# A segment mean on four engines: the instruction order comes from a list scheduler run at build time instead of from slots written by hand

## The chip, the cores and the metric

The kernel runs on one core of a Trainium2 chip. The metric is the device time of one execution in microseconds (us); smaller is better. Engines are named as in the profile: DVE is the VectorE, ACT the ScalarE, POOL the GpSimd, SP the engine whose queue starts the loads, PE the TensorE (hardly used here). "Busy" does not count instructions that only wait, branch or start a transfer. Every engine has its own list of instructions, written when the program is built. In the three traces that were set beside it (the changed kernel, `lat_p35`, `l6p35`) POOL's 90 gathers and ACT's 180 sums come in the order of that list, as far as the trace tells them apart, and an engine whose next instruction is not ready stands idle.

## The reference

```python
def setup_inputs():
    n = 10_000_000
    num_segments = 10000
    return {"data": np.random.randn(n).astype(np.float32),
            "segment_ids": np.sort(np.random.randint(0, num_segments, n))}     # int64

def reference(data, segment_ids):
    num_segments = int(segment_ids.max()) + 1
    sums = np.zeros(num_segments, dtype=np.float32)
    counts = np.zeros(num_segments, dtype=np.float32)
    np.add.at(sums, segment_ids, data)
    np.add.at(counts, segment_ids, 1)
    return sums / np.maximum(counts, 1)
```

The ids are sorted, so a segment is a contiguous stretch of about 1,000 values. The kernel does not have to read the 80 MB of ids, only to find where they change.

## The kernel before

The values lie as 128 partitions of 78,125. A partition is worked off in 90 "rows" of 875 columns (the last is shorter). A row of a partition normally holds one place where the id changes, its *cut*. Two instructions do the work on each row:

```python
def total(r):                                  # ACT: the sum of the row
    ...
    nc.scalar.activation(out=junk_a[:, 0:n], in_=d, func=ACT.Copy, accum_out=t)

def split(r):                                  # DVE: the sum of what lies before the cut
    ...
    nc.vector.scalar_tensor_tensor(
        out=junk_v[:, 0:n], in0=iota[:, 0:n], scalar=KK[:, r : r + 1], in1=d,
        op0=ALU.is_lt, op1=ALU.mult, accum_out=A[:, r : r + 1])
```

The data come in 45 tiles of two rows (875 KB each), through 18 buffers; a buffer is free when both `total` and `split` of its two rows have run. `split(r)` needs the cut `KK[:, r]`, and finding the cuts is a chain through three engines and the transfers:

1. A small load (a "probe") brings every 175th id of an even row, and DVE computes from it which stretch of 175 ids holds the change (`probes_of`, which writes the address `IDX`).
2. POOL gathers those 175 ids of each partition (`gather`, an indirect DMA into one of 18 ring slots).
3. ACT sums them (`add_ids`).
4. DVE turns the sum into the cuts of the even rows (`even_cut`).
5. The cut of an odd row is sought halfway between the cuts of its even neighbours: DVE computes that address (`between`, which writes `IDXO`),
6. POOL gathers 208 ids there, ACT sums them, and DVE writes the odd cuts (`odd_cut`).

```python
def even_cut(a, b):
    def s1():
        add_ids(asked[False, b - 1] + 1)       # ACT sums all gathers up to this one
        nc.vector.scalar_tensor_tensor(out=rows_of(a, b), in0=YY[:, a:b], scalar=float(S // K),
                                       in1=GS[:, a:b], op0=ALU.mult, op1=ALU.subtract)
    ...
def between(c, d):
    def s1(): nc.vector.tensor_add(out=SM[:, c:d], in0=rows_of(c, d), in1=rows_of(c + 1, d + 1))
    def s2(): nc.vector.scalar_tensor_tensor(out=IDXO[:, c:d], in0=SM[:, c:d], scalar=0.5,
                                             in1=FB[:, c:d], op0=ALU.mult, op1=ALU.add)
    ...
def odd_cut(c, d):
    def s1():
        add_ids(asked[True, d - 1] + 1)
        nc.vector.tensor_sub(out=KK[:, 2 * c + 1 : 2 * d : 2], in0=YO[:, c:d], in1=GSO[:, c:d])
```

The even rows are handled in nine groups, `EVEN = [3, 3, 3, 3, 6, 6, 6, 6, 6]`, with the odd rows between them; seven late rows are done by step 1 to 4 alone. In the kernel before, all of these steps are put into slots behind given rows, by hand:

```python
def chain(k):
    c, d = odds(k)
    e, b = even_cut(bounds[k], bounds[k + 1]), between(c, d)
    return e + b[:2] + [lambda: gather(True, c, d)] + b[2:]
...
put(11, chain(3), 4)                           # from row 11, four steps a row
put(13, ask(4, 3, 6))                          # gathers of even rows, in blocks of three
...
for k in range(4, NG):
    b = 2 * bounds[k]
    ...
        put(b - 24, ask(k, 0, 3))
        put(b - 19, ask(k, 3, 6))
    if k >= 5:
        put(b - 9, chain(k), 3)
    put(b - 2, odd_cut(c, c + 3))
    put(b + (1 if k == NG - 1 else 3), odd_cut(c + 3, d))
...
for r in range(-3 - X_DATA, NR):               # the loop that writes the program
    while moves and moves[0][0] <= r + X_DATA: ...      # loads, 26 rows ahead
    if r >= 0:
        add_ids(due(r))                        # sums that a rough rule takes to be there
    while nt < NR and nt <= r + ahead(r):
        total(nt); nt += 1
    if r >= 0:
        split(r)
    for f in after[r]:
        f()
```

## Time and profile before

| | before |
|---|---|
| time, median of three runs (range) | 200.46 us (199.81 to 201.47) |
| span of the profiled execution | 199.7 us |
| busy DVE / ACT / POOL | 143.1 / 138.2 / 99.7 us |
| transfers | full until about 160 us |
| DVE work still to do at 160 us | 31.7 us |

From the page of the kernel before, the busy totals and the rows that show the span in 40 slices of 5 us (a digit is the busy share of a slice in tenths):

```profile
PE 1.6 (1%) x6; PEld 1.4 (1%) x6; DVE 143.1 (72%) x501; ACT 138.2 (69%) x362; POOL 99.7 (50%) x121
...
DVE  6415387931865832979396999994689999949991
...
DMA  5999999999999999999999999999999954000000
```

No engine is full. The transfers are, until slice 32 (about 160 us), and DVE is full only after that: it fell behind while the data came in. The windows view of the same kernel gives this in numbers. Its columns are: window, length, busy us (and instructions) of PE, PEld, DVE, ACT and POOL, granted clock, mean share of the DMA engines, GB/s read.

```profile
0.00:27.00 27.00, 0.00 (x0) 0.00 (x0) 12.47 (x66) 16.79 (x35) 17.53 (x36) 1.00 0.98 237
...
60.00:100.00 40.00, 0.99 (x4) 0.93 (x4) 25.31 (x90) 27.96 (x80) 23.49 (x25) 1.00 1.06 368
100.00:130.00 30.00, 0.00 (x0) 0.00 (x0) 27.77 (x96) 24.44 (x69) 15.94 (x16) 1.00 1.05 372
130.00:160.00 30.00, 0.00 (x0) 0.00 (x0) 24.46 (x77) 20.33 (x55) 14.57 (x15) 1.00 1.01 401
160.00:215.00 55.00, 0.59 (x2) 0.50 (x2) 31.70 (x100) 28.12 (x70) 12.34 (x16) 1.00 0.10 26
```

The DMA share is at about 1 in every window to 160 us, and DVE is busy 77.5 of the 100 us between 60 and 160 (25.31 + 27.77 + 24.46). The waits view says what the engines were waiting for (engine, tile and line, the releaser, then us in total, times, longest):

```profile
POOL GT L342 <- ACT junk_a L445: 40.4, 9, 10.5
ACT junk_a L356 <- DMA GT<-in_segment_ids_dram,IDXO: 28.2, 16, 5.9
...
DVE q L437 <- ACT junk_a L356: 13.0, 4, 4.7
DVE q L437 <- issue: 10.6, 3, 7.0
DVE q L368 <- ACT junk_a L356: 9.5, 6, 4.9
...
DVE q L437 <- ACT junk_a L445: 4.0, 1, 4.0
```

L342 is the gather, L356 the id sum, L445 `total`, L368 and L437 the even and the odd cut. POOL stood 40 us before gathers, ACT stood 28 us before gathered ids that had not landed, and DVE stood 37.7 us in some 15 waits before cuts (the four lines shown, and 0.6 more).

Where ACT really waited for a gather (20 of the 90), the time from the start of POOL's gather to the start of the sum was 6.64 us in the median, by the timelines of POOL and ACT. POOL itself is busy only 1.0 us with a gather and starts the next 1.30 us after it. The Trainium skill ("Perfetto Trace Analysis", DMA Instruction — SWDGE (GPSIMD)) explains why these two differ: the profiler ends such an instruction when its descriptors are written, not when the data have moved. This trace agrees: 1.0 us against 6.64.

### The profile page before, as it was taken

To read this page: it belongs to the slowest core of one execution; us is meant where nothing else is said; L and a number is where in the kernel's file an instruction comes from. 1 tells how busy PE (TensorE), PEld (TensorE's weight loads), DVE (VectorE), ACT (ScalarE), POOL (GpSimd) and SP (SyncE) were. 2 spreads that over 40 slices of the span, in tenths; PEclk is the share of its full clock that TensorE was granted. 3 is DMA by queue.
4 is the path that set the end of the run, shared out by engine and by line. 5 is a ranking of instruction groups with operands and counts; after the bars stand their busy time and mean duration, and the time that the engine had idled before them with its cause. 6 is when DMAs were issued, how large, how long until landed. Compare 5 with 4: busy or idle time off the path is not lost.

```text
span 199.7 us, 1544 instructions
## 1 busy us (share of the span) xinstructions
PE 1.6 (1%) x6; PEld 1.4 (1%) x6; DVE 143.1 (72%) x501; ACT 138.2 (69%) x362; POOL 99.7 (50%) x121
## 2 busy tenths in 40 slices
PE   0000000000000010000000000000000000010000
PEld 0000000000000010000000000000000000010000
DVE  6415387931865832979396999994689999949991
ACT  8556387444946935988499949694996199899900
POOL 5675745750376277617770776367403778602000
DMA  5999999999999999999999999999999954000000
GB/s 67 301 270 289 273 291 195 300 259 333 349 345 350 363 345 360 354 348 412 401 405 399 332 335 358 405 412 406 402 411 423 358 151 124 11 0 2 0 0 11
DMA packets 49781, 55.67 MB, mean 279 GB/s; under 512 B 39632, under 2 KB 40200, under 8 KB 49767
## 3 DMA queue, kind: packets, MB, share of 16 engines
q1 hardware_dynamic: 43835, 40.33, 62.2%
q0 software_dynamic: 5760, 15.22, 23.4%
q14 instruction: 14, 0.11, 0.2%
q10 hardware_dynamic: 172, 0.00, 0.0%
HBM read 57.81 MB, written 0.04 MB: 290 GB/s over the span
## 4 chain that ended last, share of the span: by engine, by line
issue 28%; DMA 24%; SPq 19%; DVE 15%; ACT 9%; POOL 3%; POOLq 0%; ACTq 0%; DVEq 0%
SPq L163 14%; DMA GT<-in_segment_ids_dram,IDXO 10%; DMA data_t<-in_data_dram 10%; DVE junk_v L450 8%; SPq L178 6%; ACT junk_a L356 4%; ACT junk_a L445 4%; DMA GT<-in_segment_ids_dram,IDX 4%; POOL GT L342 3%; DVE sel L781 0%; DVE sel L772 0%; DVE most L869 0%; DVE PS L686 0%; DVE FFP L714 0%; DVE add L861 0%
## 5 line engine op out<-in xcount | busy, mean ns | idle before, releaser
L450 DVE SCALAR_TENSOR_TENSOR junk_v<-iota,q,data_t 128x875 bf16<-128x875 f32 x90 | 100.3, 1115 | 0.3
L445 ACT ACTIVATE junk_a<-data_t 128x875 bf16<-128x875 f32 x90 | 83.6, 929 | 17.7 <-DMA data_t<-in_data_dram 14.3
L342 POOL DMA_INDIRECT GT<-in_segment_ids_dram,IDXO x41 | 41.3, 1007 | 54.5 <-ACT junk_a L445 39.1
L342 POOL DMA_INDIRECT GT<-in_segment_ids_dram,IDX x49 | 49.3, 1005 | 17.8 <-issue 12.4
L356 ACT ACTIVATE junk_a<-GT 128x175 bf16<-128x175 int32 (+1 forms) x90 | 33.5, 372 | 33.2 <-DMA GT<-in_segment_ids_dram,IDXO 28.2
L437 DVE TENSOR_TENSOR q<-YO,GSO 128x3 f32<-128x3 f32 (+1 forms) x14 | 2.3, 162 | 27.6 <-ACT junk_a L356 13.0
L356 ACT ACTIVATION_READ_ACCUMULATOR junk_a<-GT 128x1 f32 x90 | 16.8, 187 | 0.0
L445 ACT ACTIVATION_READ_ACCUMULATOR junk_a<-data_t 128x1 f32 x90 | 16.8, 186 | 0.0
L368 DVE SCALAR_TENSOR_TENSOR q<-YY,GS 128x6 f32<-128x6 f32 (+1 forms) x9 | 1.5, 164 | 10.2 <-ACT junk_a L356 9.5
L450 DVE DVE_READ_ACCUMULATOR junk_v<-iota,q,data_t 128x1 f32 x90 | 7.4, 83 | 0.0
L295 DVE CAST VV<-pr 128x12 f32<-128x12 int32 (+1 forms) x9 | 1.7, 185 | 6.1 <-DMA pr<-in_segment_ids_dram 6.1
L861 POOL TENSOR_TENSOR xa<-pa,RG 128x528 f32<-128x528 f32 x1 | 1.3, 1251 | 8.3 <-DVE RG L858 8.3
L194 ACT ACTIVATE GT<-q 128x3744 int32<-128x3744 f32 x1 | 3.5, 3527 | 0.0
L708 DVE TENSOR_TENSOR q<-T,q 128x44 f32<-128x44 f32 (+3 forms) x4 | 0.7, 181 | 3.4 <-ACT junk_a L445 3.3
L311 DVE TENSOR_SCALAR FE<-ST 128x6 f32<-128x6 f32 (+2 forms) x10 | 1.9, 191 | 0.2
L320 DVE SCALAR_TENSOR_TENSOR IDX<-ST,wb 128x6 int32<-128x6 f32 (+2 forms) x11 | 1.7, 161 | 0.2
L194 ACT ACT_TABLE_LOAD x1 | 1.3, 1283 | 0.7 <-PEq L1070 0.7
L374 DVE TENSOR_SCALAR q<-q 128x6 f32<-128x6 f32 (+1 forms) x9 | 1.5, 171 | 0.3
L416 DVE TENSOR_TENSOR SM<-q 128x6 f32<-128x6 f32 (+2 forms) x9 | 1.5, 165 | 0.3
L325 DVE SCALAR_TENSOR_TENSOR YY<-ST,SG 128x6 f32<-128x6 f32 (+2 forms) x10 | 1.7, 170 | 0.0
L316 DVE TENSOR_TENSOR ST<-ST,FE 128x6 f32<-128x6 f32 (+2 forms) x10 | 1.6, 160 | 0.1
L427 DVE SCALAR_TENSOR_TENSOR YO<-VV,SR 128x6 f32<-128x6 f32 (+2 forms) x9 | 1.5, 171 | 0.2
(151 smaller groups left out, 62.2 us busy)
## 6 DMA issues: line engine op xcount, KB each, us to landing
data_t<-in_data_dram SPq DMA_DIRECT2D x44, 875.0 KB
GT<-in_segment_ids_dram,IDX POOLq DMA_INDIRECT x49
pr<-in_segment_ids_dram SPq DMA_DIRECT2D x42, 6.0 KB
GT<-in_segment_ids_dram,IDXO POOLq DMA_INDIRECT x41
data_t<-in_data_dram SPq DMA_DIRECT2D x1, 437.5 KB
data_t<-in_data_dram SPq DMA_DIRECT2D x1, 125.0 KB
out_dram<-OUT SPq DMA_DIRECT2D x1, 36.6 KB
pt<-in_segment_ids_dram SPq DMA_DIRECT2D x2, 11.0 KB
```

What stands on the lines that cost most here:

```text
L163: nc.sync.dma_start(out=pr[:, a:b, :], in_=bass.AP(ids_p.tensor, ids_p.offset + 2 * L * a, [list(ids_p.ap[0]), [2 * L, b - a], [S, K + 1]]),)
L178: nc.sync.dma_start(out=d[:, 0 : c - a], in_=data_p[:, a:c])
L194: nc.scalar.activation(out=gt32[:, :, 0 : 2 * WO : 2], in_=view(q5[:, 0, 0:1], [[0, RING], [0, WO]]), func=ACT.Copy)
L295: v.tensor_copy(out=VV[:, 2 * a : 2 * b].rearrange("p (a b) -> p a b", b=2), in_=pr32[:, a:b, 0 : 2 * K + 1 : 2 * K],)
L311: v.tensor_scalar(out=FE[:, a:b], in0=ST[:, a:b], scalar1=0.0, scalar2=FAR, op0=ALU.is_equal, op1=ALU.mult)
L320: v.scalar_tensor_tensor(out=IDX[:, c:d], in0=ST[:, c:d], scalar=float(w), in1=wb[:, c:d], op0=ALU.mult, op1=ALU.add)
L325: v.scalar_tensor_tensor(out=YY[:, a:b], in0=ST[:, a:b], scalar=float(K + 1), in1=SG[:, a:b], op0=ALU.mult, op1=ALU.add)
L342: nc.gpsimd.indirect_dma_start(out=GT[:, len(asked) % RING, 0:n], out_offset=None, in_=ids2d[:], in_offset=bass.IndirectOffsetOnAxis(ap=id ...
L356: nc.scalar.activation(out=junk_a[:, 0:n], in_=gt32[:, i % RING, 0 : 2 * n : 2], func=ACT.Copy, accum_out=to[:, r : r + 1],)
L437: nc.vector.tensor_sub(out=KK[:, 2 * c + 1 : 2 * d : 2], in0=YO[:, c:d], in1=GSO[:, c:d])
L445: nc.scalar.activation(out=junk_a[:, 0:n], in_=d, func=ACT.Copy, accum_out=t)
L450: nc.vector.scalar_tensor_tensor(out=junk_v[:, 0:n], in0=iota[:, 0:n], scalar=KK[:, r : r + 1], in1=d, op0=ALU.is_lt, op1=ALU.mult, accum_ ...
```

## The change

The slots go. The program is now described as tasks (engine, busy time, dependences, a rank that says how urgent it is, and for transfers the time of moving the bytes), and a class `Plan` steps a clock through a model of the core while the program is built. Whenever a model engine is free, it takes the most urgent task that is ready *in the model*; the order in which tasks are taken becomes the order of the program. The intent is to let the scheduler find the interleaving of even and odd gathers, id sums and cuts that hand-written slots had only approximated. The instructions themselves keep their shapes.

```diff
-    asked = {}
-    summed = []
...
+class Plan:
+    STEP = 0.025
...
+        free = {"V": 4.0, "A": 6.2, "P": 3.0, "S": 0.75}
+        pipes = {"S": deque(), "P": deque()}
...
+            def begin(n):
+                e, busy, late, _, _, _, moves = tasks[n]
+                out.append(n)
+                free[e] = now + busy
+                if moves:
+                    pipes[e].append([n, moves, now + 1.2])
+                else:
+                    heapq.heappush(events, (now + late, len(out), n))
...
+            active = [e for e in pipes if pipes[e] and pipes[e][0][2] <= now]
+            for e in active:
+                pipes[e][0][1] -= self.STEP * 0.985 / len(active)
+                if pipes[e][0][1] <= 0:
+                    heapq.heappush(events, (now + 1.25, len(out), pipes[e].popleft()[0]))
...
-    put(11, chain(3), 4)
-    put(13, ask(4, 3, 6))
... (and the other slots)
+        key = 2 * a - 10                                     # a, b: the even rows of group k
...
+        for i in range(a, b):
+            asks.append((2 * a - 10 + (i - a) * 0.1, False, i, ("E", k, 5)))   # even gathers
...
+                asks.append((2 * i - 4, True, i, ("C", k, 3)))                 # odd gathers
...
+    asks.sort()
...
+    for n, (_, odd, i, dep) in enumerate(asks):
+        deps = [dep] + [("id",) + asks[n - RING][1:3]] * (n >= RING)
+        plan.add(("ask", odd, i), "P", 1.3, deps, n, ..., moves=0.47 if odd else 0.4)
+        plan.add(("id", odd, i), "A", 0.52 if odd else 0.48, [("ask", odd, i)], n - 1000, ...)
...
+    for n in plan.order():
+        plan.tasks[n][5]()
```

Loads ("S") and gathers ("P") are two pipes. When both have something to move, each gets half of the rate; the first bytes move 1.2 us after the start, and a transfer counts as landed 1.25 us after its last byte. For a gather beside a load that makes about 1.2 + 2 x 0.40 + 1.25 = 3.3 us from start to landing. The rank `n - 1000` puts an id sum ahead of everything else on ACT as soon as the model says that its ids are there.

## The prediction

> **What bounds the kernel now.** No engine is full over the 199.7 us span (page: DVE 143.1 us busy, ACT 138.2, POOL 99.7).
> - *To 160 us the transfers are full*: the windows view shows a DMA share of 1.04 and 379 GB/s in 60–160 us. The last data tile lands by about 160; after that only ten gathers move, the last issued at 168.6.
> - *Meanwhile DVE falls behind*: busy 12.5 of the first 27 us, 21.4 of 27–60, 77.5 of 60–160. At 160 it still owes 31.7 us of work, so the kernel ends 40 us after its data.
> - *Why*: in the waits view POOL's gathers wait 40.4 us, nine times, for ACT totals: the slots put the DVE steps that compute the odd addresses behind in-order ACT and DVE work. ACT waits 28.2 us for odd gathers, DVE about 37 us for cuts (q at L437 and L368). A gather costs POOL 1.31 us; 90 are 118 us, so the stalls make POOL end at 169.6 instead of about 130.
>
> **What the change does.** No work is added or removed: compute engines keep the same instructions and shapes. Only order moves. Gathers are interleaved odd and even by need instead of in blocks of 3 or 6; id sums on ACT go ahead of totals; DVE's address steps come as soon as their inputs exist. Loads keep nearly their order.
>
> **Costing.** Transfer floor: same bytes at full rate. The ten late gathers (about 180 KB each at 405 GB/s, 4 us) move under the data; the dip to 331–357 GB/s at 110–125 us should vanish (about 2.4 us). So the last data lands near 161–162. From the split of row 88 to the end took 6.5 us: an end of about 168 if DVE has caught up. DVE floor: the start is a dependency chain which the new order hardly shortens (first odd cut still about 26 us), so about 131 us of DVE work remains at 27 us: 158 without a wait, plus 4.3 us for the store: 162. Both floors are close, so leftover waits count.
>
> I expect waits of 8–12 us. The scheduler's model lets a gather's sum start about 3.4 us after its issue; the trace shows 6.5–7.9 us (issued 52.6, summed 59.4; issued 68.5, summed 76.1). The Trainium skill ("DMA: Bandwidth & Descriptors", Queues, rings and completion order) says that an engine round-robins between queue rows by packets; this trace agrees that gathers wait among the data. ACT will stall where a sum is placed too early, but such a slip is paid once, not at every gather, since everything behind it shifts too.
>
> **Prediction: 175 us, 8 in 10 within 168.5 to 186.** Faster by over 2%: 0.94; within 2%: 0.05; slower: 0.01.
>
> **What would show it.** POOL's waits on ACT fall from 40 us to under 15; the last gather is issued before 150; DVE busy in 60–160 us rises to over 88; DVE's waits for cuts fall below 15 us; last data still at 160–163; DVE work left at 160 under 14 us; busy sums unchanged within 2 us.
>
> **What would make it wrong.** The optimistic gather latency makes ACT stall many times in the chain (even sum, cut, odd gather, odd sum): 185 or more. DVE bunches small steps ahead of splits and frees buffers late, so loads stall and the data ends after 165. Or the transfers, better fed, end earlier: below 169.

## The result, and the profile after

| | before | after |
|---|---|---|
| time, median of four runs (range) | 200.97 us (199.81 to 201.73) | 213.54 us (213.3 to 214.11) |
| ratio to before (95%) | | 1.0635 (1.0573 to 1.0697) |
| span of the profiled execution | 199.7 us | 212.3 us |
| DVE idle in the span (span less busy) | 56.6 us | 69.6 us |

Ratios, here and below, are the mean time of one kernel's runs over the mean of the other's in the same rounds, so they are not quite the ratio of the medians quoted. Executions over 1.5% slower than the fastest of the same kernel are left out of the means. The kernel became 6% slower.

From the page of the changed kernel, the lines that answer to those above (a slice is now 5.3 us):

```profile
PE 1.6 (1%) x6; PEld 1.4 (1%) x6; DVE 142.7 (67%) x501; ACT 138.2 (65%) x362; POOL 99.6 (47%) x121
...
DVE  6425083849904945974391789937927999987992
...
DMA  5999999999999999999999999999993000330000
```

The work is the same to 0.4 us on each engine, and the transfers end where they did: slice 29 or so, 160 us. The idle time of DVE rose by 13.0 us, which is the loss (the spans differ by 12.6, the busy time by 0.4 the other way). The windows view of the changed kernel:

```profile
0.00:27.00 27.00, 0.00 (x0) 0.00 (x0) 10.37 (x61) 14.76 (x29) 14.42 (x33) 1.00 0.95 229
...
60.00:100.00 40.00, 0.98 (x4) 0.93 (x4) 22.39 (x76) 28.54 (x86) 26.20 (x28) 1.00 1.05 367
100.00:130.00 30.00, 0.00 (x0) 0.00 (x0) 19.80 (x65) 20.76 (x58) 15.49 (x16) 1.00 1.04 369
130.00:160.00 30.00, 0.00 (x0) 0.00 (x0) 21.26 (x69) 22.70 (x62) 13.51 (x14) 1.00 1.02 407
160.00:215.00 55.00, 0.59 (x2) 0.50 (x2) 44.58 (x142) 34.50 (x80) 12.21 (x15) 1.00 0.09 27
```

Between 60 and 160 us DVE did 63.5 us of work where the kernel before did 77.5, and 44.6 us were left when the data had all come. The waits view of the changed kernel shows what it stood for (L412 gather, L423 id sum, L433, L449 and L500 even, late and odd cut):

```profile
DVE q L433 <- ACT junk_a L423: 34.2, 9, 7.3
ACT junk_a L423 <- DMA GT<-in_segment_ids_dram,IDX: 32.5, 19, 5.4
POOL GT L412 <- DVE IDX L394: 22.8, 1, 22.8
ACT junk_a L423 <- DMA GT<-in_segment_ids_dram,IDXO: 22.4, 17, 4.0
DVE q L500 <- ACT junk_a L423: 21.3, 6, 5.6
...
DVE q L449 <- ACT junk_a L423: 1.9, 2, 1.2
```

POOL's waits for `total`, 40.4 us before, are gone as intended; they were 3.3 us now. In their place DVE waits 57.4 us for cuts (34.2 + 21.3 + 1.9), in 17 waits of 3.4 us in the mean, and each ends with an id sum on ACT. ACT in turn stands before those sums for gathers: 36 times, 54.9 us. POOL's one wait of 22.8 us is for the address of the late rows, which DVE, by then far behind, reaches at 178 us; it falls into the time when DVE is full anyway.

The source view of the changed kernel's gather line gives the time that the gathers took (minimum, median, maximum of all):

```profile
DMA to landing us min/median/max: 2.5/6.7/8.5
```

The model has 3.3. From start to sum where ACT waited (36 gathers), the median is 6.84 us; between 50 and 160 us all lie between 6.4 and 8.6. Only the gathers after 178 us, when no loads move, are near the model: 3.1 us for the two that ACT waited for (the same view, from 170 us on, has 2.5 to 3.1 us to landing for these seven). The prediction cited the Trainium skill for DMA engines that take turns between queues by packets. (The trace before, which the prediction says agrees, has no unloaded gather to compare with.) The two numbers fit it, 3.1 us without loads and 6.4 to 8.6 among them, but they show only that a gather takes longer beside loads; no run here shows that taking turns, and not some other effect of busy transfers, is the reason.

### The scheduler's clock beside the trace

Since the order comes from a model with a clock, the model can be asked when it meant each task to start. A copy of the scheduler that prints its clock while building, set beside the trace, gives for the first odd gather of each of the nine groups:

```
group                               0     1     2     3     4     5     6      7      8
start in the scheduler's model   15.3  21.8  29.7  39.4  52.4  70.5  86.2  105.3  118.7
start on the chip                20.2  28.5  38.5  51.3  67.1  88.2 107.4  130.7  148.6
slip                              4.9   6.7   8.8  11.9  14.7  17.7  21.2   25.4   29.9
```

The slip grows by 3.1 us per group in the mean (25.0 over eight steps). It is never made up, and after the last group it stays: row 69 is split 34.2 us late, row 87 33.0 us late. The model believed that the program would end at 174.55 us; the trace ends at 212.3.

One step can be followed in the timeline of POOL in the changed kernel (start, duration, then in brackets the idle time before). The gathers of even rows (IDX) of group 6 end with the one at 95.98; the first odd one (IDXO) of that group is the last line:

```profile
95.98 1.00 POOL L412 DMA_INDIRECT GT<-in_segment_ids_dram,IDX  x1 [0.30 <-issue]
97.28 0.99 POOL L412 DMA_INDIRECT GT<-in_segment_ids_dram,IDXO  x1 [0.30 <-ACT junk_a L423]
98.58 1.00 POOL L412 DMA_INDIRECT GT<-in_segment_ids_dram,IDX  x1 [0.30 <-ACT junk_a L423]
...
102.49 1.00 POOL L412 DMA_INDIRECT GT<-in_segment_ids_dram,IDX  x1 [0.30 <-ACT junk_a L508]
107.39 1.00 POOL L412 DMA_INDIRECT GT<-in_segment_ids_dram,IDXO  x1 [3.90 <-DVE SR L488]
```

The sum of that last even gather on ACT, and the even cut on DVE that waits for it:

```profile
103.94 0.36 ACT L423 ACTIVATE junk_a<-GT 128x175 bf16<-128x175 int32 x1
104.42 0.17 DVE L433 SCALAR_TENSOR_TENSOR q<-YY,GS 128x6 f32<-128x6 f32 x1 [3.22 <-ACT junk_a L423]
```

In the model the two gathers are 7.8 us apart: gather 3.3, sum, cut, address. The scheduler filled that gap exactly, with five other gathers of 1.30 us each (97.28 to 102.49). On the chip the same steps took 11.4 us, because the sum started 8.0 us after its gather, and DVE stood 3.2 us before the cut. So POOL ran out of gathers 3.6 us too early (3.90 less the usual 0.30), with the gathers of the next group standing behind the blocked one. The next group therefore starts late by what this one lost, and loses its own part again.

### The profile page after: what moved, and what is told of

The parts are those of the page before. It is cut to its first block, busy times and chain, and to the rows that moved or that the text cites. A ratio compares the mean times of both kernels' runs of the same rounds, so it can differ in the third digit from the quotient of the medians.

```text
span 212.3 us, 1523 instructions
## 1 busy us (share of the span) xinstructions
PE 1.6 (1%) x6; PEld 1.4 (1%) x6; DVE 142.7 (67%) x501; ACT 138.2 (65%) x362; POOL 99.6 (47%) x121
## 3 DMA queue, kind: packets, MB, share of 16 engines
q0 software_dynamic: 5760, 15.22, 21.2%
## 4 chain that ended last, share of the span: by engine, by line
issue 25%; DMA 22%; SPq 21%; DVE 15%; POOL 8%; ACT 5%; POOLq 0%; ACTq 0%; DVEq 0%
SPq L237 14%; DMA GT<-in_segment_ids_dram,IDXO 10%; POOL GT L412 8%; DVE junk_v L513 8%; DMA GT<-in_segment_ids_dram,IDX 8%; SPq L252 7%; DMA data_t<-in_data_dram 4%; ACT junk_a L508 3%; ACT junk_a L423 2%; POOLq L412 0%; DVE shf L859 0%; DVE most L932 0%; DVE pa L888 0%; DVE add L924 0%; POOL pb L890 0%
## 5 line engine op out<-in xcount | busy, mean ns | idle before, releaser
L412 POOL DMA_INDIRECT GT<-in_segment_ids_dram,IDX x49 | 49.3, 1007 | 51.6 <-DVE IDX L394 22.8
L423 ACT ACTIVATE junk_a<-GT 128x175 bf16<-128x175 int32 (+1 forms) x90 | 33.4, 372 | 56.8 <-DMA GT<-in_segment_ids_dram,IDX 32.5
L412 POOL DMA_INDIRECT GT<-in_segment_ids_dram,IDXO x41 | 41.1, 1002 | 39.1 <-DVE SR L488 14.6
L433 DVE SCALAR_TENSOR_TENSOR q<-YY,GS 128x6 f32<-128x6 f32 (+1 forms) x9 | 1.5, 166 | 34.2 <-ACT junk_a L423 34.2
L423 ACT ACTIVATION_READ_ACCUMULATOR junk_a<-GT 128x1 f32 x90 | 16.8, 186 | 0.0
L500 DVE TENSOR_TENSOR q<-YO,GSO 128x3 f32<-128x3 f32 (+1 forms) x14 | 2.2, 160 | 21.4 <-ACT junk_a L423 21.3
L326 DVE CAST jj<-jj_i 128x128 f32<-128x128 int32 x1 | 1.5, 1485 | 0.7 <-POOL jj_i L325 0.7
L891 POOL TENSOR_SCALAR pb<-pb 128x168 f32<-128x168 f32 (+1 forms) x2 | 1.6, 787 | 0.2
## 6 DMA issues: line engine op xcount, KB each, us to landing
data_t<-in_data_dram SPq DMA_DIRECT2D x1, 437.5 KB, 14.8
```

The source lines that it names most:

```text
L412: nc.gpsimd.indirect_dma_start(out=GT[:, i % RING, 0:n], out_offset=None, in_=ids2d[:], in_offset=bass.IndirectOffsetOnAxis(ap=idx[:, r : ...
L423: nc.scalar.activation(out=junk_a[:, 0:n], in_=gt32[:, i % RING, 0 : 2 * n : 2], func=ACT.Copy, accum_out=to[:, r : r + 1],)
```

## The experiments

**Theory A**: the model lets a gather be summed about 3.5 us too early. The scheduler spaces everything so that the tasks just fit the model's latencies. On the chip each group (even gather, sum, cut, odd gather) overruns by about that error, and because all three engines run in order, what is lost in one group is added to the next: about nine times 3.5 us, not once.

**Rival B**: the order is poor in itself (id sums before totals, DVE's small steps before splits, even and odd gathers mixed), and would be so with a correct model too.

**Later rivals**: only one engine's order carries the loss (ACT's, DVE's or POOL's), or the slack can be bought by ranks instead of by a correct model.

Each kernel below is the changed kernel with one edit, but for `half_before`, which is the kernel before. All were timed in three rounds against the kernel before on the same chip (its median was 201.0 to 203.0 us there), and all gave the right result but the two `half_` kernels.

### The landing constant of gathers, four sizes

```diff
-                    heapq.heappush(events, (now + 1.25, len(out), pipes[e].popleft()[0]))
+                    heapq.heappush(events, (now + (4.75 if e == "P" else 1.25), len(out), pipes[e].popleft()[0]))
```

`lat_p35` is this edit: the model's gather latency becomes 6.8 us, as in the traces. `lat_m1`, `lat_p175` and `lat_p7` have 0.00, 3.00 and 8.25 in place of 4.75.

> Only the constant in the scheduler's model that says how long after its bytes a gather counts as landed is raised, from 1.25 to 4.75 us, so that a gather takes about 6.8 us in the model as the trace of the changed kernel shows (median 6.84 us over the 36 gathers that ACT waited for). Theory A (the error of 3.5 us is paid again at every gather hop, about ten steps of 3 to 4 us): the slip of the rows against the scheduler's own clock stops growing (it grew from 5.5 to 34 us), the waits of DVE on even and odd cuts fall from 55 us to under 20, and the time falls to 177 to 188 us, faster than before. Theory B (the order itself is bad: gathers taken one by one, small steps bunched, the last rows' addresses late): the same rules make the order, so the time stays at 205 us or more.

> Half of the correction: the landing constant is 3.00 us in place of 1.25, so a gather counts 5.05 us. Theory A: the error left is about 1.8 us a hop, so about half of the gain over the changed kernel: 190 to 202 us. Theory B: 205 us or more.

> The error made larger: the landing constant is 0, so a gather counts about 2.0 us and the error is 4.8 us a hop in place of 3.5. Theory A: about ten hops of 1.25 us more, so 220 to 230 us. Theory B: within 3 us of the changed kernel's 213.5.

> Too long on purpose: the landing constant is 8.25 us, so a gather counts about 10.3 us. Theory A: sums are placed later than needed, no engine waits for a gather, and only slack is lost: within 6 us of the corrected kernel, 178 to 192 us. Theory B: 205 us or more.

Measured:

| kernel | model's gather latency, us | end by the scheduler's clock | span on the chip | time, median us (range) | ratio to before (95%) |
|---|---|---|---|---|---|
| `lat_m1` | 2.0 | 174.7 | 225.0 | 225.84 (223.86 to 226.92) | 1.1234 (1.1124 to 1.1344) |
| after | 3.3 | 174.6 | 212.3 | 213.54 (213.3 to 214.11) | 1.0635 (1.0573 to 1.0697) |
| `lat_p175` | 5.05 | 174.9 | 196.3 | 198.99 (198.13 to 200.03) | 0.9943 (0.9869 to 1.0016) |
| `lat_p35` | 6.8 | 174.9 | 192.3 | 193.44 (191.2 to 194.07) | 0.9611 (0.9517 to 0.9706) |
| `lat_p7` | 10.3 | 178.7 | 188.0 | 189.61 (189.05 to 190.68) | 0.9464 (0.9387 to 0.954) |

The ends by the scheduler's clock are its own claim, not times of the chip. They show that the longer latency costs the schedule nothing when the scheduler knows of it: 174.6 to 174.9 for the first four. What moves is how far the chip falls behind the claim: 50, 38, 21 and 17 us. `lat_m1`, `lat_p175` and `lat_p7` came where they were expected. Theory A is borne out in its direction, and in its size while the model is far too short: from 2.0 to 3.3 us of latency the time falls by 12.3 us (9.8 us per us, the step being 1.25 us; by the ratios, since the changed kernel was timed in another set, 12.0), and from 3.3 to 5.05 by 14.6 us (8.3 per us). A single wait could not give a slope of eight to ten; nine groups can. From 5.05 to 6.8 it falls by only 5.5 us (3.2 per us).

The slip of the first odd gathers shows the same thing more directly. From the first group to the last it grows by 36.7 us in `lat_m1` (4.6 us a step, the model being 4.8 too short), by 25.0 in the changed kernel (3.1 a step; 3.5 too short) and by 13.6 in `lat_p175` (1.7 a step; 1.8 too short). In the first two it grows at every step. In `lat_p175` 6.2 of the 13.6 us come in one step, so that one fits in its mean only. Rival B, which needed 205 us or more for `lat_p35`, falls.

Two things do not fit the simple form. `lat_p35` was expected at 177 to 188 and came at 193.4; and giving the model 3.5 us *more* than the chip needs helped again, by 3.8 us. The waits view of `lat_p35` shows what DVE still waits for:

```profile
DVE VV L369 <- DMA pr<-in_segment_ids_dram: 12.2, 4, 4.6
DVE q L500 <- issue: 12.1, 5, 5.1
DVE q L500 <- ACT junk_a L423: 10.4, 4, 8.0
DVE q L433 <- ACT junk_a L423: 4.7, 2, 4.5
```

DVE's waits for cuts fell from 57.4 to 27.6 us (the three lines of L500 and L433, and 0.4 more), not to under 20 as expected. The 12.2 us before probes are new on the chip but not a new error of the model: by the scheduler's own clock the last probes of groups 1 to 4 land at 11.6, 15.1, 21.2 and 33.2 us, and DVE took them up at 10.8, 16.6, 22.5 and 35.1, at most 1.9 us later.

The larger loss is on ACT. The slip of the first odd gathers in this kernel is 0.2 to 3.0 us up to group 4, then steps to 7.6 and to 14.2, and both steps lie at stretches in which ACT idles before instruction after instruction. The brackets name no other engine and no transfer as the cause (here "remote"; in other lines "issue" or ACT itself):

```profile
76.18 0.36 ACT L423 ACTIVATE junk_a<-GT 128x175 bf16<-128x175 int32 x1 [1.65 <-remote]
78.27 0.93 ACT L508 ACTIVATE junk_a<-data_t 128x875 bf16<-128x875 f32 x1 [1.64 <-remote]
```

Such gaps of over 0.5 us add up to 4.9 us between 71 and 79 us and to 6.3 us between 98 and 108, and ACT's slip against the scheduler's clock goes from 3.4 to 8.0 and from 7.7 to 13.4 there. `lat_p175` has such a stretch too (62 to 74 us, slip of ACT from 4.7 to 11.1: the one large step above), and `lat_p7` has gaps of 12 us in all; the changed kernel, `lead12`, `l6p35` and `l12p7` below have none. What causes them stays open. If they hold up the whole chain, as the steps in the slip suggest, `lat_p175`, `lat_p35` and `lat_p7` are slower than the latency alone would make them, and the slopes beyond 3.3 us are not the latency's alone.

### One engine's order alone, or two

Both schedules are computed, with the shipped constant and with 4.75, and each engine's order is taken from one or the other; the merge keeps all dependences.

```diff
+    def merged(self, engines, lag):
+        tight, loose = self.order(), self.order(lag)
+        ...
+        for e in "VAPS":
+            queues[e] = deque(n for n in (loose if e in engines else tight) if self.tasks[n][0] == e)
+        ...
-    for n in plan.order():
+    for n in plan.merged("V", 4.75):
```

`hyb_V` takes DVE's order from the corrected schedule, `hyb_A` ACT's, `hyb_P` POOL's, `hyb_VA` and `hyb_VP` those of two engines.

> The changed kernel's order on ACT and GpSimd, but DVE's own order taken from the scheduler with the corrected gather latency (the run that gave 193.4 us). It tells on which engine the slip is paid. If DVE pays it (too little split work stands between the step that writes a gather's addresses and the step that uses its sum): most of the 20 us gain comes with DVE alone, 193 to 203 us. If ACT's place for the sums pays it: 208 us or more.

> The mirror of the run before: DVE and GpSimd in the changed kernel's order, ACT's own order taken from the scheduler with the corrected latency. If DVE pays the slip: 207 us or more. If ACT pays it (a sum stands in front of totals that could run, so ACT idles): 193 to 203 us.

> DVE's and ACT's order from the scheduler with the corrected latency (4.75 us), GpSimd's gathers in the changed kernel's order. Theory A' (the loop is closed in GpSimd's queue, which still has 2 to 6 gathers between even and odd): at least half of the 20 us gain is missing, 203 to 216 us. If ACT and DVE pay: 190 to 200 us.

> Only GpSimd's gathers stand in the order of the corrected schedule (4 to 8 of them between even and odd); DVE and ACT keep the changed kernel's order. If the order of the gathers alone is what was wrong: 193 to 203 us. If the three orders have to fit each other (DVE and ACT then wait for sums in an order in which they do not come): 210 us or more.

> GpSimd's and DVE's order from the corrected schedule, ACT in the changed kernel's order. If the loop runs through GpSimd and DVE, and ACT only has to keep up: 192 to 203 us. If ACT's sums, which stand too early in front of totals, cost by themselves: 207 us or more.

| kernel | corrected order on | time, median us | ratio to before (95%) |
|---|---|---|---|
| `hyb_V` | DVE | 211.96 | 1.0526 (1.0441 to 1.0612) |
| `hyb_VP` | DVE, POOL | 217.05 | 1.0688 (1.0641 to 1.0735) |
| `hyb_VA` | DVE, ACT | 221.32 | 1.0987 (1.0938 to 1.1036) |
| `hyb_P` | POOL | 229.04 | 1.1161 (1.1098 to 1.1225) |
| `hyb_A` | ACT | 234.18 | 1.1628 (1.151 to 1.1745) |
| `lat_p35` | all | 193.44 | 0.9611 (0.9517 to 0.9706) |

`hyb_V` and `hyb_A` each came in the range that was to blame the other engine, `hyb_VA` was slower than either of its ranges, and `hyb_VP` fell in the range that was to blame ACT's sums. Only `hyb_P` met a reading that fits all five: the three orders have to fit each other. No engine's order gives most of the gain, no pair that I ran does, and four of the five are slower than the changed kernel. The order of one engine is only right beside the others of the same schedule. In `hyb_A`, for example, the order of the sums no longer fits what POOL does when, and one wait of ACT for a gather reaches 10.2 us:

```profile
ACT junk_a L440 <- DMA GT<-in_segment_ids_dram,IDX: 57.2, 16, 10.2
DVE q L517 <- ACT junk_a L440: 28.1, 3, 13.4
```

So the loss cannot be given to one queue. My reading of the POOL timeline above, that POOL's queue closes the loop from group to group, is one view of a loop that goes through all three; these runs neither single it out nor exclude it.

### Half the bytes on the transfers, the schedule untouched

Each data tile loads only one row's 875 columns, and both of its rows read them. The result is wrong, the instructions and their order stay (but for the last tile, which takes one load instead of two).

```diff
-        nc.sync.dma_start(out=d[:, 0 : c - a], in_=data_p[:, a:c])
-        if c < b:
-            nc.sync.dma_start(out=d[:, c - a : b - a], in_=data_p[:, c:b])
+        nc.sync.dma_start(out=d[:, 0:L], in_=data_p[:, a : a + L])
...
-        d = tiles[r // 2][:, (r % 2) * L : (r % 2) * L + n]
+        d = tiles[r // 2][:, 0:n]
```

`half_after` does this to the changed kernel, `half_before` to the kernel before. The point: if the model is wrong because gathers queue among loads, then fewer loads should bring the chip nearer to the model.

> Wrong result on purpose: the changed kernel, schedule untouched, but each data tile loads only one row's columns and both of its rows read them, so the data's bytes are halved and the same compute instructions run. If a gather is late because its packets queue among the data's, its time from issue to sum falls from 6.8 us to under 5.5 after the first 50 us, DVE's waits for cuts fall from 55 us to under 30, and the time to 180 to 195 us. If the 6.8 us belong to the gather itself (descriptors, issue), they stay at 6 or more and the time stays above 203 us.

> Wrong result on purpose: the same halved data for the kernel before. It is the control: how much the hand-written slots gain from half the data. If the handwritten order has the slack for a late gather, it gains less than the changed kernel, at most 15 us: 185 to 200 us.

`half_after` took 201.64 us (ratio to before 0.9994, 0.9912 to 1.0076), `half_before` 186.96 us (0.9278, 0.9207 to 0.9349). So the changed kernel gained 12 us, less than expected, and the kernel before gained 14 to 15, so the control gained no less. DVE's waits for cuts in `half_after` were 44.1 us, not under 30. The pair of times settles nothing. The traces say more. The DMA row of `half_after` is:

```profile
DMA  5999999999999999888647767884740002220000
```

The loads run up to 18 tiles ahead, so the transfers stay full to slice 15 (80 us) and only then thin out. Accordingly the gathers where ACT waited still took 4.7 to 6.6 us up to 57 us, and 3.6 to 4.9 between 100 and 140 us. And the slip of the first odd gathers against the scheduler's clock, which grew by 3 to 4.5 us per group in the last four steps of the changed kernel, reads:

```
group            0    1    2    3    4     5     6     7     8
half_after     4.5  4.8  5.8  9.3  12.3  13.8  18.5  19.9  21.0
```

In the last two steps, where gathers take 3.6 to 5 us, it grows by only 1.4 and 1.1 us. That fits Theory A. The step before them does not: from group 5 to 6 (84 to 105 us) it grew by 4.7 us. ACT stood 4.1 us there in gaps like those of `lat_p35`, so the step says little either way. The lever was blunt besides, because the buffers kept the transfers full for the first 80 us, and it also fed both kernels' data earlier, which the control shows to be worth as much.

### Slack bought with ranks, the model left wrong

If the slip comes from too few gathers between a group's last even gather and its first odd one, then asking for the even gathers earlier should help though the latency in the model stays wrong. `lead12` ranks a group's even gathers and address steps 12 rows earlier:

```diff
-        key = 2 * a - 10
+        key = 2 * a - 22
...
-        key += 3
+        key += 15
...
-            asks.append((2 * a - 10 + (i - a) * 0.1, False, i, ("E", k, 5)))
+            asks.append((2 * a - 22 + (i - a) * 0.1, False, i, ("E", k, 5)))
```

> The scheduler's model keeps its too short gather latency of 3.3 us. Only the priorities change: a group's even gathers and the address steps before them are ranked twelve rows earlier. In the order that is built, 6, 8, 8, 12, 3, 11, 13, 7, 3 gathers then stand on GpSimd between the last even gather of a group and its first odd one, in place of 2, 3, 3, 2, 3, 5, 5, 6, 1. Theory A' (each group pays once what the gathers standing between do not cover of about 9 us from the last even gather to the odd address, because GpSimd's queue is in order and the next group stands behind): the slip of the gathers against the scheduler's clock falls from 30 us to under 15 and the time to 190 to 203 us. If it is where ACT and DVE place the sum and the cut that costs, the model's latency being still wrong: 208 us or more.

It took 200.67 us (ratio to before 0.9963, 0.992 to 1.0006): 13 us less than the changed kernel, with the same wrong latency, and in the expected range; the slip ended at 15.2 us, just over the 15 expected. The gathers that stand on POOL between a group's last even and first odd gather, and the slip of the first odd gather:

```
group                      0    1    2    3    4    5    6    7    8
gathers between, after     2    3    3    2    3    5    5    6    1
gathers between, lead12    6    8    8   12    3   11   13    7    3
slip, after              4.9  6.7  8.8 11.9 14.7 17.7 21.2 25.4 29.9
slip, lead12             4.6  4.5  4.5  5.8  8.9  8.9  8.9  8.9 15.2
```

The slip stands still in the groups with seven or more gathers between (1, 2, 5, 6 and 7; group 3, with twelve, adds 1.3 us) and grows by 3.1 and 6.3 us in the two with three (4 and 8). Eight gathers take 8 x 1.30 = 10.4 us, about what the chain through sum, cut and address took on the chip in the group shown above (11.4 us). DVE still waited 43.3 us for cuts in it, so slack for POOL alone is not all.

### Both together

`l6p35` has the constant 4.75 and ranks the even gathers 6 rows earlier (keys `2 * a - 16`, `key += 9`); `l12p7` has 8.25 and 12 rows (`2 * a - 22`, `key += 15`), to see whether still more slack pays.

> An attempt at a better version: the corrected latency (4.75 us) and the even gathers ranked six rows earlier. Theory A': no worse than the corrected kernel's 193.4, 184 to 194 us. The transfers still end near 161 us and set a floor near 170.

> An attempt at a better version: the landing constant of 8.25 us (which alone gave 189.6 us) and the even gathers ranked twelve rows earlier, so that 6 to 13 gathers stand between even and odd in every group. Theory A': 181 to 190 us, no group waiting over 2 us on GpSimd.

`l6p35` took **183.33 us** (183.31 to 184.41), ratio to before 0.9127 (0.908 to 0.9174), the best of all and better than both kernels. `l12p7` took 188.25 us (0.935, 0.9288 to 0.9411): more slack costs something again, and its schedule is longer already by the scheduler's clock (179.6 us, against 172.6 for `l6p35`). The slip of the first odd gathers in `l6p35` is 1.4, 1.3, 1.4, 1.3, 3.0, 3.0, 3.0, 4.5 and 3.7 us. Its windows after 60 us, and its waits for cuts:

```profile
60.00:100.00 40.00, 0.98 (x4) 0.93 (x4) 29.97 (x105) 33.44 (x98) 30.55 (x32) 1.00 1.06 361
100.00:130.00 30.00, 0.00 (x0) 0.00 (x0) 29.33 (x89) 26.77 (x69) 13.79 (x14) 1.00 1.05 372
130.00:160.00 30.00, 0.59 (x2) 0.50 (x2) 28.27 (x92) 24.54 (x66) 17.85 (x20) 1.00 1.02 408
160.00:215.00 55.00, 0.00 (x0) 0.00 (x0) 15.53 (x51) 12.36 (x28) 1.25 (x1) 1.00 0.06 22
```

```profile
DVE q L433 <- ACT junk_a L423: 12.6, 2, 8.4
...
DVE q L500 <- ACT junk_a L423: 2.9, 4, 1.2
...
DVE q L449 <- ACT junk_a L423: 2.4, 1, 2.4
```

DVE is busy 87.6 of the 100 us from 60 to 160 and has 15.5 us of work left, and the waits for cuts are 17.9 us. That is nearly the picture that the prediction had drawn for the change itself. How much of the 10 us from `lat_p35` to `l6p35` the earlier ranks gave is not shown: `l6p35` has none of ACT's unexplained gaps, and the two stretches in `lat_p35` had cost about as much (ACT's slip grew by 4.6 and 5.7 us in them). In POOL's timeline of `l6p35` ten gathers stand between the last even gather of group 6 (80.30 us) and the first odd one, which does not wait beyond the usual 0.30:

```profile
94.61 1.00 POOL L412 DMA_INDIRECT GT<-in_segment_ids_dram,IDXO  x1 [0.30 <-DVE base L631]
```

## Why the prediction was right or wrong

The prediction was 175 us (168.5 to 186) and faster; the kernel came to 213.5 and slower.

**Right.** The transfers bound the first 160 us and did not get shorter or longer: last data at 160 to 161. No work was added; the busy sums agree to 0.4 us. The gather latency that the scheduler assumes, about half of what the trace of the kernel before shows, was seen and written down, and the first sentence under "what would make the prediction wrong" is what happened.

**The step that failed** is: "such a slip is paid once, not at every gather, since everything behind it shifts too". It would hold if the first late gather moved the whole plan as one block. But the error is one of a duration, not of a start. After the shift, the next group again needs 3.5 us more than the plan leaves between its even gather and its odd address, and the shift has not given it any. The trace shows the slip growing by 3.1 us in the mean at each of the eight steps between groups, the landing constants of 0.00, 1.25 and 3.00 us give 8 to 10 us of time per us of error, and the corrected model gains 20 us with the same ranks. The "waits of 8–12 us" were this step's number. Taken to the sum of the prediction: 131 us of DVE work after 27 us, and about 15 us of everything else up to 175 (a span of 173.2). Measured, DVE had 132.3 us of work after 27 us and stood idle for 53.0 of the remaining 185.3. This term alone is 38 us too small, and so is the prediction.

**Wrong with it**, each from the views named: DVE busy between 60 and 160 us was 63.5, not over 88; its waits for cuts 57.4 us, not under 15; its work left at 160 us 44.6, not under 14; the last gather was issued at 188.3 us, not before 150. POOL's waits for ACT did fall, from 42 to 18 us (14.8 for sums, 3.3 for totals; predicted under 15), but POOL waited 51 us for steps of DVE instead (22.8 + 14.6 + 8.9 + 3.1 + 2.0 in the waits view, most of them address steps, and 22.8 the late rows' wait that falls into the time when DVE is full; 7 us before). The wait had only moved on to another engine of the same loop.

**Two smaller points.** The prediction took the start as unchanged; DVE did 10.4 us of work in the first 27 instead of 12.5, so 2 of the 13 us were lost there. And the dip of the transfers at 110 to 125 us, expected to vanish with the blocks of gathers, stayed: the page of the changed kernel has two slices of 318 and 320 GB/s at 117 to 127 us, and `l6p35` three of 323 to 343 at 118 to 132. It stayed with each of these orders of the gathers; what it comes from was not tried.

**Still open.** Which of the three queues carries the slip from group to group (mixed orders could not show it); ACT's gaps in `lat_p35`, `lat_p175`, `lat_p7` and `half_after`; and what makes up the remaining 9 us between the claim of `l6p35`'s schedule (172.6) and its span (181.6). DVE waits 12.4 us for probes in it, 10.9 of them in the first 27 us, but it takes up the probes of groups 1 to 5 at most 2.6 us later than the schedule has it.

## What to carry to other kernels

A static order made by a scheduler is only as good as the durations in its model, and an optimistic latency on a path that is passed again and again is paid at every pass: count the passes and multiply, and do not assume that the rest of the plan simply shifts. Take each latency from a trace of the loaded program, and prefer one that is too long: here 3.5 us too little cost 20 us, and 3.5 us too much cost nothing that shows (189.6 against 193.4 us, both with ACT's gaps). To see where a schedule goes wrong, print the scheduler's own start times, set them beside the trace, and look at where the difference grows.

## What the Trainium skill lacked or had wrong

- "DMA: Bandwidth & Descriptors", Anatomy of one DMA — SWDGE (gpsimd) path, fits a transfer from the gpsimd queue as 2.0 us plus bytes at 436 GB/s. For an even gather (128 x 175 ids of 8 bytes, 179 KB) that gives an estimate of 2.4 us. Without loads that is near: 2.5 to 3.1 us to landing here, and 3.1 us from start to sum. Beside full loads it is far off: a median of 6.84 us from start to sum (up to 8.6). The fit itself has no term for other traffic. With the loads thinned out (`half_after`, between 100 and 140 us) it was 3.6 to 4.9 us. These runs do not show which effect of busy transfers is the reason.
- "GPSIMD Engine Reference" says to use the engine for gathers but has no figure for issuing one ("DMA: Bandwidth & Descriptors" has about 1 us to the first byte on this path). In these traces a gather of 128 x 175 or 128 x 208 ids keeps POOL busy for 1.00 us, and gathers in a row start every 1.30 us, which here decides how many fit into a wait.
- No page speaks of how the error of a schedule's model adds up across engines that run in order. Here it was 8 to 10 us of time per us of error in one latency, as long as the model was at least 1.8 us too short. "Perfetto Trace Analysis", Identifying Dependency Chains, says to look at the semaphores that an instruction waits on; the last of those waits names the right engine here, but not that the same loss recurs in each of nine groups.
